# A four-layer hybrid trunk on one core: one-half norms and gating moved into PSUM, layer norm on VectorE alone, low halves gathered, and another final norm

## The chip, the cores and the metric

The kernel runs on one core of a Trainium2 chip. A core has a matrix engine (TensorE, PE in the profile, with its weight loads listed as PEld), a vector engine (VectorE, DVE), an activation engine (ScalarE, ACT), a general engine (GpSimd, POOL) and a queue engine (SyncE, SP). Each engine works through its own instructions in order. The metric is the device time of the kernel in microseconds (us), the median of several runs, lower is better.

## The reference

One inference step of a four-layer trunk with model width 1024, for a prompt of 512 positions and a sample group of 8 x 4 = 32 positions that share the weights. Each layer is a token mixer and a SwiGLU block, each with a norm ahead of it and a residual around it:

```python
for i in range(4):
    h = rmsnorm(x, norm_mix[i])
    # i=0 pooling, i=1 Conformer convolution (31 taps), i=2 gating MLP, i=3 gated short conv
    x = x + mixer_i(h)
    x = x + silu(gate) * up @ w_out        # gate, up = split(rmsnorm(x, norm_ffn[i]) @ w_in)
y = rmsnorm(x, norm_final)

def rmsnorm(x, g): return x * rsqrt(mean(x * x) + 1e-6) * g

def conv(h):                               # layer 1
    a, gate = split(h @ w_in + b_in)
    c = depthwise_causal(a * sigmoid(gate), dw) + dw_b
    return silu(layernorm(c)) @ w_out

def gating(h):                             # layer 2, chunks of 128 positions, 4 groups of 256 columns
    u, v = split(gelu(h @ w_in))
    v = layernorm(v)
    mixed = tril(w_s) @ v (per chunk and group) + b_s
    return (u * mixed) @ w_out
```

Everything is float32. The outputs are y and the new states of the mixers.

## The kernel before

**Tiling.** Activations lie feature-major: 8 tiles of 128 features (NC = 8), and the 544 positions are two halves, A (256 prompt positions) and B (256 prompt and 32 sample positions). A float32 product is three single-pass matmuls: each weight tile and each activation is split into a high part, cast by ACT (`hi_...`, `H_...`, `hH_...`), and a low part, raw minus high, by DVE or POOL (`lo_...`, `L_...`, `hL_...`); per 128x128 tile PE does high x high, high x low and low x high. In layers 2 and 3 (counted from 0) the SwiGLU block's inner pairs use seven products in the place of eight (`seven`).

**Order.** `Stream` holds the steps (one weight column each: loads, matmuls, evacuation) and writes every engine's instructions by hand: ahead of a step's matmuls the casts of weights up to four slots and the low halves up to three slots ahead; behind them one stage of each pending evacuation (generators: each `yield` is the end of a stage), then the side generators (the norms that are prepared), then background jobs (pool mixer, convolution taps, layer norm) as far as a cost model of DVE and POOL (`Timed`) says that they fit beside PE. A step with `flush` first writes out all pending evacuations. Raw weights come by SP's queue. A weight load with `share=True` has its low half on POOL unless the model finds POOL behind, with `share=0` on DVE; with `sum=True` ACT writes the negated high half and a DMA issued by POOL adds the raw weight from memory onto it (lines 173 to 178).

**PSUM** has eight banks, and every tile there is one bank, taken in turn (`PS`). SBUF tiles of 288 columns come from one pool (`T`).

**The norms** (lines 437 to 561). ACT squares each x tile, the squares are added over the eight tiles (`add_square`), matmuls with a column of ones sum over features into `st_...`, and `rsqrt_` makes the inverse root on a few columns by an integer first step and two polynomial steps. Where one half alone is normed (`twin`), part of its operands lie in PSUM, with three copies. `rp_...` matmuls spread the result over all partitions. `factor` keeps it as a factor for later; `prepare` norms the tiles at once, two a stage: DVE makes `hn`, ACT casts it in that stage, DVE and POOL make the low halves a stage later.

**Where the change applies, in order of time.** SwiGLU 0 runs for half A (about 26 to 237 us); then the convolution's input for A (`conv_in`, 237 to 286), SwiGLU 0 for B, the convolution's output for A, its input for B (521 to 575), SwiGLU 1 for A, and so on. The 31 taps (`conv_taps`) are a background job on DVE in PSUM accumulators; for B, four products with row sums add the sample positions, and POOL adds their bias and gathers the sum over the channel tiles (`gather`, called a tile later). The gating layer runs from about 1004 to 1177 us: 16 columns `ps_gv` (v first, then u), transposes of v, `gm_norm` as a background job (`vT`, five blocks of positions times four groups; blocks 0 and 2 have two of their steps on POOL, `LN_POOL`), and `mix_step` for each tile and half placed among the columns by `GM_A` and `GM_B`: matmuls `mix`, then `mix_evac` (`gy` = mix + bias, times u, cast to `H_gy`, and `L_gy` a stage later). `out_proj` for A then begins (`ps_go`). The last SwiGLU block takes its last two output columns (`tail=2`) first for A and then for B, so that A's final norm (`final`) runs beside B's columns; A's result tiles `y` are made by POOL, B's by DVE, and go out by SP's and ACT's queues.

Of the kernel before, what the change touches and what calls it, by code (L numbers as in the profile page):

```python
# [10 lines left out]
I32 = mybir.dt.int32  # L11
# [4 lines left out]
P = 128  # L16
# [55 lines left out]
def trunk_kernel(  # L72
# [364 lines left out]
    def rsqrt_(ms, wv, tv, twin=None):  # L437


        wp, tp = twin or (wv, tv)  # L440
# [5 lines left out]
        dve.tensor_scalar(tv.bitcast(I32), ms.bitcast(I32), 1, None, op0=ALU.logical_shift_right)  # L446
        dve.tensor_scalar(wv.bitcast(I32), tv.bitcast(I32), -1, 0x5F3759DF, op0=ALU.mult, op1=ALU.add)
# [14 lines left out]
    def token_rsqrt(acc, halves, name, lag, mid=(None,)):  # L462
# [8 lines left out]
        twin = (ps[:, 8 + b0 : 8 + b1], ps[:, 16 + b0 : 16 + b1]) if len(halves) == 1 else None  # L471
# [10 lines left out]
        for rows, c0, c1 in ((P, b0, min(b1, 4)), (NS, 4, b1)):  # L482
            if c1 > c0:
                dve.tensor_scalar(
                    ms[:rows, c0:c1], ps[:rows, c0:c1], 1.0 / D, EPS, op0=ALU.mult, op1=ALU.add
                )
        rsqrt_(*(t[:, b0:b1] for t in (ms, rs, tv)), twin)
# [13 lines left out]
    class Norm:  # L501
# [16 lines left out]
        def add_square(self, h, c, eng):  # L518
# [4 lines left out]
            elif eng is None:  # L523
                self.acc[h] = [self.acc[h], q]
            else:
# [17 lines left out]
        def prepare(self, h, eng):  # L543
# [5 lines left out]
            for c in range(0, NC, 2):  # L549
                vs = []  # L550
                for i in (c, c + 1):
# [5 lines left out]
                    self.hs[h][i] = split(v, w, f"h_{nm}_{i}")  # L557
                    vs.append(v)
                yield
                for i, v in zip((c, c + 1), vs):  # L560
                    split_lo(self.hs[h][i], v, w, dve if i % 2 else eng)
# [146 lines left out]
    def ffn(layer, n, nxt, halves=(0, 1), rel=False, fill=None, tail=0, free=False, phases=((0, HF), (HF, NF))):  # L708

        eng = pool if rel else dve  # L710
# [3 lines left out]
        for pi, (j0, j1) in enumerate(phases):  # L714
# [101 lines left out]
            for m in range(NC):  # L816
# [3 lines left out]
                if joint and not (final_phase and m >= NC - tail):  # L820
# [8 lines left out]
            for i, (m, hs) in enumerate(seq):  # L829
                if len(hs) == 1 and tail and hs[0] == B:  # L830
# [7 lines left out]
                    S.add(lds[m][:1], lambda wt, m=m, piece=piece: piece(wt, m, 0), lambda ps: iter(()))  # L838
                    S.add(lds[m][1:], lambda wt, m=m, piece=piece: piece(wt, m, (K + 1) // 2),
# [7 lines left out]
    def out_proj(src, acts, n, name, halves=(0, 1), rel=False, fill=None, between=None):  # L847
# [8 lines left out]
        for q in range(NC // 2):  # L856
            ls = cols_of(src[q], f"{name}_{q}_{hn}", bool(rel))
            for i, l in enumerate(ls):
# [213 lines left out]
    def conv_in(h, fill):  # L1072
# [65 lines left out]
        for c in range(NC):  # L1138
            la, lg = cols_of(w_cin[c], f"ci{c}_{h}", True)
# [12 lines left out]
    def conv_taps(h, c, e, ev):  # L1152
# [23 lines left out]
        if ev is not None:  # L1176
# [9 lines left out]
            pool.tensor_scalar(cc[:, HP:w], cc[:, HP:w], col(C_DWB + c), None, op0=ALU.add)  # L1186
        dve.tensor_add(cc[:, :HP], cc[:, :HP], outs[1])

        def gather():

            if c == 0:
# [129 lines left out]
    def gm_norm():  # L1321
# [11 lines left out]
        for g in range(NG):  # L1333
            for b, (h, o, n) in enumerate(blocks):
# [3 lines left out]
                if b in LN_POOL:  # L1338
                    dve.tensor_scalar(v, v, mu, r, op0=ALU.subtract, op1=ALU.mult)
# [329 lines left out]
```

## Time and profile before

| | us |
|---|---|
| median of 3 runs | 2135.81 (2133.74 to 2137.49) |
| the profiled execution, its own time | 2138.85 |
| its span, first to last instruction | 2137.2 |
| PE busy in the span | 2107.3 |
| DVE / ACT / POOL busy | 1485.7 / 1018.5 / 646.2 |

PE is busy in almost all of the span, and the rest of the span is waits of PE and stretches of a half granted clock. A matmul's start is exact, its end is modelled. The views used below are the page, the list of who waited for whom on PE, the timeline (start, length, engine, line, operation, output<-inputs, shapes, count, and in brackets the idle time ahead and what ended it), groups of instructions (count | busy us, mean ns | idle before), and windows (busy us of PE with the number of instructions, granted clock, DMA share, GB/s). Nearly all DVE, POOL and PE instructions bear line 109, that of a helper, so they are told apart by the names of their tiles.

### The profile page before, as it was taken

To read this page: it belongs to the slowest core of one execution; us is meant where nothing else is said; L and a number is where in the kernel's file an instruction comes from. 1 tells how busy PE (TensorE), PEld (TensorE's weight loads), DVE (VectorE), ACT (ScalarE), POOL (GpSimd) and SP (SyncE) were. 2 spreads that over 40 slices of the span, in tenths; PEclk is the share of its full clock that TensorE was granted. 3 is DMA by queue.
4 is the path that set the end of the run, shared out by engine and by line. 5 is a ranking of instruction groups with operands and counts; after the bars stand their busy time and mean duration, and the time that the engine had idled before them with its cause. 6 is when DMAs were issued, how large, how long until landed. Compare 5 with 4: busy or idle time off the path is not lost.

```text
span 2137.2 us, 42390 instructions
## 1 busy us (share of the span) xinstructions
PE 2107.3 (99%) x16678; PEld 2097.1 (98%) x16678; DVE 1485.7 (70%) x3191; ACT 1018.5 (48%) x1778; POOL 646.2 (30%) x502
## 2 busy tenths in 40 slices
PE   9999999999999999999999999999999999999997
PEld 8999999999999999999989999999999999999997
DVE  7867799624999666566387767586765649585685
ACT  5445544545444654444436546354521246364463
POOL 3011587879888840000043102011000001111121
PEclk9999999999999999999999999999999999999998
DMA  7645554545956465546225646465544455575562
GB/s 237 212 155 159 180 188 145 182 145 193 188 179 193 153 203 158 173 155 192 87 75 154 155 119 155 129 152 146 136 92 91 90 139 114 133 160 132 134 150 72
DMA packets 130190, 320.81 MB, mean 150 GB/s; under 512 B 32556, under 2 KB 40328, under 8 KB 129728
## 3 DMA queue, kind: packets, MB, share of 16 engines
q1 hardware_dynamic: 110664, 279.47, 44.2%
q0 software_dynamic: 18176, 37.33, 10.7%
q8 instruction: 131, 2.15, 0.4%
q10 hardware_dynamic: 1152, 1.32, 0.2%
q14 instruction: 67, 0.55, 0.1%
HBM read 313.81 MB, written 4.62 MB: 149 GB/s over the span
## 4 chain that ended last, share of the span: by engine, by line
PE 88%; DVE 7%; ACT 2%; DMA 2%; issue 1%; POOL 0%; ACTq 0%; DVEq 0%; POOLq 0%
PE ps_o L109 24%; PE p_w L109 18%; PE ps_g L109 12%; PE ps_u L109 12%; PE ps_gv L109 3%; PE ps_co L109 2%; PE ps_sx L109 2%; PE ps_sc L109 2%; PE ps_sbg L109 2%; PE ps_so L109 2%; PE ps_cg L109 2%; PE ps_ca L109 1%; DVE ct L109 1%; DMA raw_fi<-in_w_fin 1%; PE ps_go L109 1%; PE pd L109 1%
## 5 line engine op out<-in xcount | busy, mean ns | idle before, releaser
L109 PE MATMUL ps_o<-H_p,lo_fo 128*128 128x288 f32 (+1 forms) x1408 | 349.8, 288 | 1.4 <-POOL lo_fo L109 1.4
L109 PE MATMUL ps_o<-H_p,hi_fo 128*128 128x288 f32 (+1 forms) x1408 | 350.3, 288 | 0.0
L109 PE MATMUL ps_o<-L_p,hi_fo 128*128 128x288 f32 (+1 forms) x1408 | 349.6, 288 | 0.1
L169 ACT CAST hi_fi<-raw_fi 128x1024 fp32r<-128x1024 f32 x192 | 201.0, 1049 | 126.8 <-DMA raw_fi<-in_w_fin 47.9
L109 PEld LDWEIGHTS ps_o<-H_p,lo_fo 128*128 128x128 f32 x1408 | 245.7, 188 | 1.6 <-POOL lo_fo L109 1.6
L109 PEld LDWEIGHTS ps_o<-L_p,hi_fo 128*128 128x128 f32 x1408 | 245.8, 188 | 1.4 <-DVE L_p L109 1.4
L109 PEld LDWEIGHTS ps_o<-H_p,hi_fo 128*128 128x128 f32 x1408 | 245.9, 188 | 0.2
L169 ACT CAST hi_fo<-raw_fo 128x768 fp32r<-128x768 f32 (+2 forms) x194 | 149.8, 774 | 194.3 <-PE ps_o L109 106.2
L249 POOL DMA_DIRECT2D lo_w_a<-in_w_fin x92 | 80.7, 1002 | 443.2 <-ACT lo_w_a L248 425.8
L109 POOL TENSOR_TENSOR lo_fi<-raw_fi,hi_fi 128x1024 fp32r<-128x1024 f32 (+1 forms) x86 | 203.5, 2385 | 25.9 <-PE ps_g L109 6.7
L109 DVE TENSOR_TENSOR lo_fo<-raw_fo,hi_fo 128x768 fp32r<-128x768 f32 (+3 forms) x130 | 113.8, 878 | 121.4 <-issue 69.5
L109 DVE SCALAR_TENSOR_TENSOR ct<-ce,colsT,ct 128x256 f32<-128x256 f32 x448 | 182.8, 487 | 0.0
L109 DVE TENSOR_TENSOR lo_fi<-raw_fi,hi_fi 128x1024 fp32r<-128x1024 f32 (+1 forms) x92 | 116.4, 1267 | 64.1 <-ACT t L735 17.4
L109 PE MATMUL p_w<-L_t_f,hi_w_s 128*128 128x272 f32 x432 | 124.3, 288 | 0.0
L109 PE MATMUL p_w<-H_t_f,hi_w_s 128*128 128x272 f32 x432 | 124.1, 287 | 0.0
L109 PE MATMUL p_w<-H_t_f,lo_w_s 128*128 128x272 f32 x432 | 123.9, 287 | 0.0
L109 PE MATMUL ps_g<-hH_f,hi_fi 128*128 128x256 f32 (+1 forms) x464 | 123.7, 289 | 0.0
L109 PE MATMUL ps_u<-hH_f,hi_fi 128*128 128x256 f32 (+1 forms) x464 | 123.6, 289 | 0.0
L109 PE MATMUL ps_g<-hH_f,lo_fi 128*128 128x256 f32 (+1 forms) x464 | 123.2, 288 | 0.2 <-DVE lo_fi L109 0.2
L109 PE MATMUL ps_u<-hL_f,hi_fi 128*128 128x256 f32 (+1 forms) x464 | 123.3, 288 | 0.0
L109 PE MATMUL ps_u<-hH_f,lo_fi 128*128 128x256 f32 (+1 forms) x464 | 123.2, 288 | 0.0
L109 PE MATMUL ps_g<-hL_f,hi_fi 128*128 128x256 f32 (+1 forms) x464 | 123.1, 288 | 0.0
(430 smaller groups left out, 6675.5 us busy)
## 6 DMA issues: line engine op xcount, KB each, us to landing
raw_fi<-in_w_fin SPq DMA_DIRECT2D x192, 512.0 KB, 4.4
raw_fo<-in_w_fout SPq DMA_DIRECT2D x96, 384.0 KB, 3.2
raw_w<-in_w_fin SPq DMA_DIRECT2D x72, 512.0 KB, 4.2
raw_fo<-in_w_fout SPq DMA_DIRECT2D x94, 320.0 KB, 3.2
lo_w_a<-in_w_fin POOLq DMA_DIRECT2D x92, 256.0 KB, 4.9
raw_ci<-in_w_cin SPq DMA_DIRECT2D x32, 512.0 KB, 4.6
raw_co<-in_w_cout SPq DMA_DIRECT2D x16, 512.0 KB, 4.8
raw_gi<-in_w_gin SPq DMA_DIRECT2D x16, 512.0 KB, 3.9
```

The source lines that it names most:

```text
L109: return fn(*a, **k)
L169: act.copy(self.hi, self.raw)
L249: nc.gpsimd.dma_start(self.lo, self.pair.plain(self.k)[1], accum_op=ALU.add)
```

## The change

Ten edits. **(1)** `rsqrt_`: the integer step is one instruction in the place of two; for one half it reads a copy of `ms` in PSUM. **(2)** The sums of squares of SwiGLU 0's half A are added up in a PSUM tile (`eng = "psum"`). **(3)** `prepare` casts the normed tiles a stage later, with the low halves in that same stage. **(4)** The convolution's first two input columns for A have their low halves on DVE and not as POOL's share. **(5)** The sample bias of the convolution moves from the end of the taps into `gather`. **(6)** The layer norm of the gating MLP is all on DVE, two instructions per block and group. **(7)** The gating product stays in the PSUM tile of `mix` and is cast from there. **(8)** Columns 8 to 15 of the gating input have their low halves gathered (`sum`). **(9)** The first two output columns of the gating layer for A run as a pair: `mm_pair` takes both columns tile by tile and the low weights one tile later. **(10)** The end: three columns (`tail=3`) first for A and then for B, one load each; no PSUM twin in the last norm; `idle` matmuls ahead of and behind B's statistics; A's result on DVE and later.

```diff
@@ -437,14 +437,14 @@
-        wp, tp = twin or (wv, tv)
+        wp, tp, mp = twin or (wv, tv, ms)
...
-        dve.tensor_scalar(tv.bitcast(I32), ms.bitcast(I32), 1, None, op0=ALU.logical_shift_right)
-        dve.tensor_scalar(wv.bitcast(I32), tv.bitcast(I32), -1, 0x5F3759DF, op0=ALU.mult, op1=ALU.add)
+        dve.tensor_scalar(wv.bitcast(I32), mp.bitcast(I32), -0.5, float(0x5F3759DF), op0=ALU.mult, op1=ALU.add)
         copied(wp, wv)
@@ -459,7 +459,7 @@
-    def token_rsqrt(acc, halves, name, lag, mid=(None,)):
+    def token_rsqrt(acc, halves, name, lag, mid=(None,), alone=False):
@@ -468,7 +468,9 @@
         ms, rs, tv = (sp.tile([P, 5], F32, tag=f"n{n}", name=f"{n}_{name}", bufs=2) for n in ("ms", "ri", "rt"))
-        twin = (ps[:, 8 + b0 : 8 + b1], ps[:, 16 + b0 : 16 + b1]) if len(halves) == 1 else None
+        twin = None
+        if len(halves) == 1 and not alone:
+            twin = [ps[:, o + b0 : o + b1] for o in (8, 16, 24)]
         if B in halves:
@@ -484,6 +486,8 @@
                 )
+        if twin:
+            dve.tensor_copy(twin[2], ms[:, b0:b1])
         rsqrt_(*(t[:, b0:b1] for t in (ms, rs, tv)), twin)
@@ -522,6 +526,11 @@
                 self.acc[h] = [self.acc[h], q]
+            elif eng == "psum":
+                a = self.acc[h]
+                self.acc[h] = q if c == NC - 1 else PS(f"sa_{self.name}_{h}") if c == 1 else a
+                dve.tensor_add(self.acc[h][:, :w], a[:, :w], q[:, :w])
             else:
@@ -546,19 +555,24 @@
             yield
-            for c in range(0, NC, 2):
+            last = ()
+            for c in range(0, NC + 2, 2):
+                for i, v in last:
+                    self.hs[h][i] = split(v, w, f"h_{nm}_{i}")
                 vs = []
-                for i in (c, c + 1):
+                for i in range(c, min(c + 2, NC)):
                     v = (PS if i % 2 else T)(f"hn_{nm}_{i}")[:, :w]
...
                     )
-                    self.hs[h][i] = split(v, w, f"h_{nm}_{i}")
-                    vs.append(v)
+                    vs.append((i, v))
+                for i, v in last:
+                    split_lo(self.hs[h][i], v, w, dve if i % 2 else eng)
+                last = vs
                 yield
-                for i, v in zip((c, c + 1), vs):
-                    split_lo(self.hs[h][i], v, w, dve if i % 2 else eng)
@@ -707,7 +721,7 @@
-        eng = pool if rel else dve
+        eng = pool if rel else "psum" if halves == (A,) else dve
         hn = "".join(map(str, halves))
@@ -817,7 +831,7 @@
                 cut = ((j0, ks[0]), ks)
-                if joint and not (final_phase and m >= NC - tail):
+                if joint:
                     cut = ((j0, j1),)
@@ -835,8 +849,9 @@
-                    S.add(lds[m][:1], lambda wt, m=m, piece=piece: piece(wt, m, 0), lambda ps: iter(()))
-                    S.add(lds[m][1:], lambda wt, m=m, piece=piece: piece(wt, m, (K + 1) // 2),
+                    k1 = (K + 1) // 2
+                    S.add(lds[m], lambda wt, m=m, piece=piece: piece(wt[:k1], m, 0), lambda ps: iter(()))
+                    S.add(lds[m], lambda wt, m=m, piece=piece: piece(wt[k1:], m, k1),
                           lambda ps, m=m, hs=hs: out_evac(ps, m, hs, True))
@@ -844,7 +859,7 @@
-    def out_proj(src, acts, n, name, halves=(0, 1), rel=False, fill=None, between=None):
+    def out_proj(src, acts, n, name, halves=(0, 1), rel=False, fill=None, between=None, pair=False):
         hn = "".join(map(str, halves))
@@ -855,6 +870,13 @@
             ls = cols_of(src[q], f"{name}_{q}_{hn}", bool(rel))
+            if pair and q == 0:
+                S.add(ls, lambda wt: mm_pair((wt[:NC], wt[NC:]), acts, halves, name),
+                      lambda pss: both(evac(pss[0], 0), evac(pss[1], 1)), flush=True, fill=fill)
+                for m in range(2):
+                    if between:
+                        between(m)
+                continue
             for i, l in enumerate(ls):
@@ -1136,7 +1158,7 @@
         for c in range(NC):
-            la, lg = cols_of(w_cin[c], f"ci{c}_{h}", True)
+            la, lg = cols_of(w_cin[c], f"ci{c}_{h}", h == B or c > 1)
             if c == 0:
@@ -1183,11 +1205,12 @@
                 yield 0.7
-            pool.tensor_scalar(cc[:, HP:w], cc[:, HP:w], col(C_DWB + c), None, op0=ALU.add)
         dve.tensor_add(cc[:, :HP], cc[:, :HP], outs[1])
...
+            if ev is not None:
+                pool.tensor_scalar(cc[:, HP:w], cc[:, HP:w], col(C_DWB + c), None, op0=ALU.add)
             if c == 0:
@@ -1335,13 +1358,8 @@
                 mu, r = mv[:n, b, 0:1], rs[:n, b : b + 1]
-                if b in LN_POOL:
-                    dve.tensor_scalar(v, v, mu, r, op0=ALU.subtract, op1=ALU.mult)
-                    pool.tensor_mul(v, v, lg)
-                    pool.tensor_add(v, v, lb)
-                else:
-                    dve.scalar_tensor_tensor(v, v, mu, lg, op0=ALU.subtract, op1=ALU.mult)
-                    dve.scalar_tensor_tensor(v, v, r, lb, op0=ALU.mult, op1=ALU.add)
+                dve.scalar_tensor_tensor(v, v, mu, lg, op0=ALU.subtract, op1=ALU.mult)
+                dve.scalar_tensor_tensor(v, v, r, lb, op0=ALU.mult, op1=ALU.add)
                 if b == 3:
@@ -1367,33 +1385,31 @@
         w = HW[h]
-        y = T(f"gy_{c}_{h}")
         bs = gk["bs"]
-        dve.tensor_add(
-            b3(y[:, :HP], 2), b3(pmx[:, :HP], 2), bs[:, g : g + 1, :].to_broadcast([P, 2, CH])
-        )
+        y = b3(pmx[:, :HP], 2)
+        dve.tensor_add(y, y, bs[:, g : g + 1, :].to_broadcast([P, 2, CH]))
         if h == B:
-            dve.tensor_add(
-                b3(y[:, HP:w]), b3(pmx[:, HP:w]), bs[:, g : g + 1, :DS].to_broadcast([P, DB, DS])
-            )
-        dve.tensor_mul(y[:, :w], y[:, :w], uu[h][c][:, :w])
-        gact[h][c] = split(y[:, :w], w, f"gy_{c}_{h}")
-        return y
+            y = b3(pmx[:, HP:w])
+            dve.tensor_add(y, y, bs[:, g : g + 1, :DS].to_broadcast([P, DB, DS]))
+        dve.tensor_mul(pmx[:, :w], pmx[:, :w], uu[h][c][:, :w])
+        gact[h][c] = split(pmx[:, :w], w, f"gy_{c}_{h}")
     def mix_evacs(pss, hs, c):
-        ys = {h: mix_evac(pss[h], c, h) for h in hs}
+        for h in hs:
+            mix_evac(pss[h], c, h)
         yield
         for h in hs:
-            split_lo(gact[h][c], ys[h][:, : HW[h]], HW[h], dve)
+            split_lo(gact[h][c], pss[h][:, : HW[h]], HW[h], dve)
...
     for q in range(NC):
-        for i, l in enumerate(cols_of(w_gin[q], f"gi{q}", 0)):
+        for i, l in enumerate(cols_of(w_gin[q], f"gi{q}", 0, q >= NC // 2)):
             m = 2 * q + i
@@ -1409,7 +1425,7 @@
-    out_proj(w_gout, gact, nf2, "go", (A,), rel=True, between=mix_b)
+    out_proj(w_gout, gact, nf2, "go", (A,), rel=True, between=mix_b, pair=True)
     out_proj(w_gout, gact, nf2, "go", (B,))
@@ -1499,28 +1515,43 @@
     nl = Norm(C_FIN, "nl")
-    ffn(3, nf3, nl, fill=1, tail=2, phases=JOINT)
+    ffn(3, nf3, nl, fill=1, tail=3, phases=JOINT)
...
+    def idle(n):
+        ps = PS("idle")
+        for _ in range(n):
+            pe.matmul(ps[:, :P], ones, ones, start=True, stop=True)
...
         w = HW[h]
-        out = yield from token_rsqrt(nl.acc, (h,), f"nl_{h}", [None])
+        def covered(n):
+            if h == B:
+                idle(n)
+            yield
+        if h == B:
+            idle(4)
+        out = yield from token_rsqrt(
+            nl.acc, (h,), f"nl_{h}", covered(0) if h == B else [None] * 2, mid=covered(7), alone=True
+        )
         if h == A:
-            r = T(f"r_nl_{h}")
-            scaled(r[:, :w], out[h][:, :w])
+            for _ in range(3):
+                yield
         for c in range(NC):
-            y = T(f"y_{h}_{c}")
-            if h == A:
-                pool.tensor_mul(y[:, :w], xg[h, c][:, :w], r[:, :w])
-            else:
-                dve.scalar_tensor_tensor(
-                    y[:, :w], xg[h, c][:, :w], RSQ, out[h][:, :w], op0=ALU.mult, op1=ALU.mult
-                )
+            y = T(f"y_{h}_{c}")[:, :w]
+            dve.scalar_tensor_tensor(y, xg[h, c][:, :w], RSQ, out[h][:, :w], op0=ALU.mult, op1=ALU.mult)
             q = act if h == B and c % 2 == 0 else nc.sync
-            q.dma_start(o_y[c, :, HO[h] : HO[h] + w], y[:, :w])
+            q.dma_start(o_y[c, :, HO[h] : HO[h] + w], y)
+            if h == A and c == 2:
+                yield
@@ -1537,7 +1568,6 @@
 PAIRS = (1,)
-LN_POOL = (0, 2)
 GM_A = {11: (0, 1), 12: (2, 3), 13: (4,), 14: (5, 6), 15: (7,)}
```

## The prediction, made before the changed kernel was run

> **What bounds the kernel now.** First the page, for the share of PE; then the list of who ended PE's waits; then windows around the longest of these, for the granted clock; then the timeline there, for the cause.
>
> ```profile
> PE 2107.3 (99%) x16678; PEld 2097.1 (98%) x16678; DVE 1485.7 (70%) x3191; ACT 1018.5 (48%) x1778; POOL 646.2 (30%) x502
> ```
>
> ```profile
> PE rp_nl L109 <- DVE ri_nl L109: 4.0, 2, 3.4
> PE pd L109 <- DVE ht L109: 3.9, 1, 3.9
> PE ps_go L109 <- ACT H_gy L608: 3.4, 1, 3.4
> PE mix L109 <- DVE vT L109: 2.0, 1, 2.0
> PE ps_cg L109 <- ACT ct L1083: 1.6, 1, 1.6
> PE ps_o L109 <- POOL lo_fo L109: 1.4, 1, 1.4
> ...
> PE ps_cga L109 <- ACT hH_n L530: 1.1, 1, 1.1
> ...
> PE ps_cg L109 <- DVE ct L109: 0.9, 1, 0.9
> ```
>
> ```profile
> 547.20:550.60 3.40, 1.82 (x14) 1.00 0.95 253
> 1100.10:1103.50 3.40, 3.40 (x18) 0.55 0.26 87
> 1124.00:1127.40 3.40, 3.40 (x17) 0.55 0.02 6
> 2124.10:2137.20 13.10, 3.49 (x16) 0.50 0.47 161
> ```
>
> PE is idle for 2137.2 - 2107.3 = 29.9 us in all, and the matmuls themselves stay (the pairing only reorders them). So an edit counts only where it ends one of these waits, or a stretch at half clock. The windows add a second price: behind the waits of 2.0 and 3.4 us PE had some 3.4 us at half clock (0.55 in windows a little off its edges), so each cost about another 3.4 x 0.5 = 1.7 us; the wait of 1.6 us, whose window kept 1.00, cost only itself.
>
> [...]
>
> **The change, part by part, in order of time.**
>
> *Start.* `pd` waits on the pool mixer's norm, where `rsqrt_` loses one of its small instructions, about 0.2 us apart (below). **0.2 us.**
>
> *Convolution input, A.*
>
> ```profile
> 231.68 10.03 POOL L109 TENSOR_TENSOR lo_ci<-raw_ci,hi_ci 128x1024 fp32r<-128x1024 f32 x4 [47.48 <-PE ps_o L109]
> 239.38 2.61 DVE L109 TENSOR_TENSOR sq_n<-sq_n,sq_n 128x256 f32<-128x256 f32 x1
> 540.74 5.57 DVE L109 SCALAR_TENSOR_TENSOR ct<-ce,colsT,ct 128x256 f32<-128x256 f32 x14
> 541.23 2.42 POOL L109 TENSOR_TENSOR lo_ci<-raw_ci,hi_ci 128x1024 fp32r<-128x1024 f32 x1 [0.52 <-issue]
> ```
>
> The sum of squares took 2.61 us beside POOL's low halves and ends when POOL's instruction ends; the taps, which accumulate in PSUM, took 5.57 / 14 = 0.40 us each beside the same kind of POOL instruction. So a DVE instruction on SBUF alone stands still beside POOL, and one with an operand in PSUM does not. Edits 2 and 4 take away both sides: the sums go to PSUM, and the first four low halves to DVE, 4 x 1.22 us (row `lo_gi` below, same shape). POOL's four in a row each held up one DVE instruction, this one by 2.61 - 0.45 = 2.2 us, and the last x, whose cast PE waits for, stands behind them. Counting only the last two, 4.3 us go, and the two low halves that come ahead of the last x bring 2.4: DVE is 1.9 us earlier where PE waits 1.05. **1.05 us**; if DVE were as late as now, nothing. The integer steps of edit 1 are unblocked too, but `rp_n` stands at a fixed place in PE's order, so the next wait, 0.9 us `<- DVE ct` (a bank that waits for r), stays: 0.
>
> *Convolution input, B, and SwiGLU 1, A.*
>
> ```profile
> 547.28 0.77 ACT L608 CAST H_h_f<-hn_f 128x256 fp32r<-128x256 f32 x2 [3.64 <-DVE hn_f L109]
> 656.97 0.36 POOL L109 TENSOR_SCALAR cc<-cc,colsT 128x32 f32<-128x32 f32 x1 [5.46 <-DVE cc L109]
> 657.29 6.67 POOL L109 TENSOR_TENSOR lo_fo<-raw_fo,hi_fo 128x768 fp32r<-128x768 f32 x4
> ```
>
> ACT stood 3.64 us at the cast of `hn_f`, with the sigmoid that frees PE's bank behind it. A stage later `hn_f` is long done, so ACT doesn't stop. What is late next is DVE: its low halves now share a stage with the casts and may wait for them, in a stretch where DVE has hardly a pause. Between nothing and the whole 1.6 us I take half, **0.8 us**; below nothing it could go to about -2 (each of four stages losing the 0.5 us that a cast takes to arrive). POOL stood 5.46 us at the sample bias, four low halves behind it, and PE's 1.4 us wait ended with the first. In `gather`, a tile later, the taps are done, so the bias waits for nothing: **1.4 us**.
>
> *The gating layer.*
>
> ```profile
> L109 DVE TENSOR_TENSOR lo_gi<-raw_gi,hi_gi 128x1024 fp32r<-128x1024 f32 x16 | 19.6, 1224 | 34.8 <-issue 20.5 <-PE ps_gv L109 12.8 <-PE ps_o L109 1.5
> L109 DVE TENSOR_TENSOR L_gy<-gy,H_gy 128x256 fp32r<-128x256 f32 (+1 forms) x16 | 16.9, 1057 | 5.6 <-ACT H_gy L608 5.6
> L109 DVE SCALAR_TENSOR_TENSOR vT<-vT,mv,lng 128x256 f32<-128x256 f32 (+1 forms) x12 | 9.8, 813 | 0.0
> L109 DVE TENSOR_SCALAR vT<-vT,mv,gri 128x256 f32<-128x256 f32 x8 | 3.6, 455 | 0.0
> L109 DVE TENSOR_TENSOR ps_u<-ps_u,t 128x288 f32<-128x288 f32 (+1 forms) x42 | 18.8, 446 | 31.0 <-PE ps_u L109 27.7 <-ACT t L732 3.3
> L109 DVE TENSOR_TENSOR q<-q,t 128x256 f32<-128x256 f32 (+1 forms) x60 | 26.3, 449 | 6.0 <-DVE q L109 0.9 <-ACT t L735 0.9
> L109 POOL TENSOR_TENSOR vT<-vT,lng 128x256 f32<-128x256 f32 x8 | 6.8, 844 | 82.1 <-DVE vT L109 79.6 <-issue 1.2 <-DMA out<-vT 1.2
> L109 POOL TENSOR_TENSOR lo_go<-raw_go,hi_go 128x1024 fp32r<-128x1024 f32 x8 | 19.9, 2492 | 12.1 <-ACT hi_go L169 8.4 <-PE ps_go L109 3.6
> L176 ACT ACTIVATE lo_fi<-hi_fi 128x1024 fp32r<-128x1024 f32 x16 | 16.9, 1057 | 19.9 <-issue 16.2 <-PE ps_so L109 2.5 <-PE ps_go L109 1.2
> L177 POOL DMA_DIRECT2D lo_fi<-in_w_fin x16 | 13.9, 870 | 118.7 <-ACT lo_fi L176 109.5 <-DVE x L109 9.3
> ```
>
> DVE is the late one: both waits come from its queue. It gains: the low halves of columns 14 and 15, which fall among the norm's instructions, 2 x 1.22 = 2.4 us (six more fall where DVE has pauses); `L_gy` at 0.45 for a mean of 1.06, and up to 2 us where it met `lo_go`; and the norm no longer meets 16 POOL instructions of 0.8 us. It loses: eight `vT` of 0.455 become sixteen of 0.41 to 0.81, so 8 x (0.82 - 0.455) = 2.9 up to 8 x (1.63 - 0.455) = 9.4 us. I take 4, since most of the POOL instructions that made the 0.81 are gone. `lo_go` stays on POOL and will meet the norm instead of `L_gy`; so up to the first wait (1097.5 us) the gain is the 2.4, plus about 3 for the norm's and gating's stalls, less 5/8 of the 4: about 3 us, against the 2.0 that PE waits. Up to the second, 1.6 us more from the `L_gy` just ahead of it and the rest of the stalls, together some 5; and the pair lets PE do 40 instead of 21 matmuls, 19 x 0.126 = 2.4 us more (2107.3 us by 16678 matmuls), before it needs the last `H_gy`. That is 7.4 us of cover for the 3.4. So both waits and both half-clock stretches go: 2.0 + 1.7 + 3.4 + 1.7 = **8.8 us**; the first has only about 1 us in hand. The gathered columns cost ACT 8 x 1.06 and POOL 8 x 0.87 us, both off the path: a column's low half is begun three columns of 48 x 0.126 = 6.0 us ahead.
>
> [...]
>
> *The end.*
>
> ```profile
> 1.13 6.11 PE L109 MATMUL warm<-ones 128*128 128x128 f32 x40 [1.13 <-DVE ones L109]
> 2118.30 0.16 DVE L109 TENSOR_SCALAR ms_nl<-st_nl 128x2 f32<-128x2 f32 x1 [1.52 <-PE st_nl L109]
> 2120.91 0.71 PE L109 MATMUL rp_nl<-ident,ri_nl 128*128 128x128 f32 x4 [0.57 <-DVE ri_nl L109]
> 2122.12 0.29 PE L109 MATMUL ps_o<-H_p,lo_fo 128*128 128x288 f32 x1
> 2123.09 0.45 DVE L109 TENSOR_TENSOR x<-ps_o,x 128x288 f32<-128x288 f32 x1
> 2124.06 1.75 PE L109 MATMUL st_nl<-ones,sq_nl 128*128 128x1 f32 x10 [0.46 <-ACT sq_nl L516]
> 2129.25 1.78 PE L109 MATMUL rp_nl<-ident,ri_nl 128*128 128x128 f32 x6 [3.44 <-DVE ri_nl L109]
> 2131.07 3.01 DVE L109 SCALAR_TENSOR_TENSOR y<-xg,rp_nl 128x288 f32<-128x288 f32 x8 [1.87 <-PE rp_nl L109]
> ```
>
> The last column ends at 2122.12 + 0.29 = 2122.41; from there 14.8 us to the end of the span. To the statistics 1.65: the residual started 0.68 late on DVE; with A's chain over earlier it is about 1.0, but four `idle` matmuls of 6.11 / 20 = 0.31 stand ahead, so 1.2. Statistics 1.75 at half clock, about 1.0 when `idle` holds the clock. Chain 3.44 for 13 instructions: A's twelve took 2120.91 - 2118.30 = 2.61, 0.22 each; ten remain and no POOL stands beside them, 2.2, plus 0.2 since A's last five `y` precede them on DVE. The seven `idle` matmuls, 2.1, fit beside that. Spreading 1.82, about 1.0 at full clock. The results and their way out, 6.1, stay. 1.2 + 1.0 + 2.4 + 1.0 + 6.1 = 11.7, so 3.1 us less; and A's 0.57 us wait goes, its spreading now two pieces of a column later. **3.6 us.**
>
> **Sum.** 0.2 + 1.05 + 0.8 + 1.4 + 8.8 + 3.6 = 15.85 us, from the profiled 2138.85 to 2123.0. The median of the runs is 2135.81, 3.04 below the profiled execution; with the same distance the forecast is 2120.0.
>
> **Rivals.** *The norm keeps DVE late.* With `lo_go` on POOL beside a longer norm, the first wait stays (only it: 15.85 - 3.7 = 12.15, 2123.7 us) or both (7.05, 2128.8). For it: only about 1 us in hand. Against the second: cover twice its need. *PSUM doesn't shield.* If the cast and low halves from PSUM stand still as those from SBUF do, gating and convolution A win nothing: 0.2 + 0.8 + 1.4 + 3.6 = 6.0, 2129.8 us. The taps' 0.40 speak against it. *Other waits fill in*, within 0.2% (4.3 us, about what a measurement here can tell from no change): new waits of 12 us or more, say DVE late in the convolution, 2133. *Slower: the gathered halves come late.* PE needs a column's low half at its third matmul, so each of eight columns can stall. They have 18 us; ACT's 1.06, POOL's 0.87 and a transfer must fit. It decides from 18 on: 1.8 us beyond, with half clock behind each wait, 8 x 3.5 = 28 us against the 15.85, so about 2148. Against it: the windows show the DMA engines at 0.02 to 0.26 in that stage.
>
> **How the numbers follow.** Forecast 0.62 (2115.5 to 2122.5: banks and small waits that also go, or 2.5 us of the end or of the convolution not won), first gating wait stays 0.13, both stay 0.07, no shield 0.05, filled in 0.07, slower 0.06. The range of 8 in 10 goes from 2115.5 to 2127.5: the forecast, the next case and part of the third. Faster by over 0.2%: 0.62 + 0.13 + 0.07 + 0.05 = 0.87; within 0.07; slower 0.06.
>
> **What would show it.** Right: no PE wait on `H_gy`, `vT`, `lo_fo` or `hH_n`, granted clock 1.00 from 1090 to 1130 us and up to the last `rp_nl`, `L_gy` near 0.45 us, some 12 us from the last `ps_o` to the end of the span, and the 0.9 us wait on `ct` still there. Wrong: a PE wait on `lo_gi`, on `L_gy` or `L_h`, or a `mix` that still waits on `vT`; `idle` matmuls that hold up `rp_nl`.

## The result, and the profile after

The changed kernel takes 2125.09 us (median of 6 runs, 2120.3 to 2130.03) beside 2137.59 us for the kernel before in the same rounds (6 runs, 2133.74 to 2142.48): a ratio of 0.9939, 95% interval 0.9925 to 0.9952. A second set of rounds on another occasion gave 2122.61 (6 runs) beside 2133.91 (11 runs), again 0.9939 (0.992 to 0.9958). The forecast was 2120.0 in a range of 2115.5 to 2127.5, so the time lies inside the range and the gain is 12.5 us where 15.85 was forecast. The profiled execution took 2125.66, its span 2124.0; 13.2 us of span went, and the profiles tell where.

The page of the changed kernel, its line of busy times:

```profile
PE 2105.0 (99%) x16700; PEld 2096.3 (99%) x16700; DVE 1450.7 (68%) x3186; ACT 1021.6 (48%) x1783; POOL 617.9 (29%) x482
```

PE has 22 matmuls more, the 11 `idle` ones in two passes each, and is idle for 2124.0 - 2105.0 = 19.0 us, before 29.9. Who ended its waits (us in total, times, longest):

```profile
PE mix L109 <- DVE vT L109: 2.4, 2, 2.2
PE ps_g L109 <- ACT hi_fi L169: 2.4, 1, 2.4
PE pd L109 <- DVE ht L109: 2.1, 1, 2.1
...
PE ps_cg L109 <- DVE ct L109: 0.9, 1, 0.9
...
PE ps_g L109 <- DVE lo_fi L109: 0.8, 1, 0.8
...
PE rp_nl L109 <- DVE ri_nl L109: 0.2, 1, 0.2
...
PE ps_go L109 <- ACT H_gy L622: 0.2, 1, 0.2
```

The waits on `hH_n`, `ct` by ACT and `lo_fo` are gone, that on `H_gy` is 0.2 for 3.4, those on `ri_nl` are 0.2 for 4.0, and the 0.9 on `ct` by DVE is still there: as forecast, but for the 0.2 us on `H_gy`. The wait of `mix` on `vT`, which was to go, is 2.4 for 2.0. Windows of the changed kernel (its columns as before) around the start, the gating layer and the end:

```profile
57.00:60.20 3.20, 0.82 (x5) 0.42 (x3) 0.51 (x1) 1.59 (x3) 0.00 (x0) 0.99 0.70 277
60.20:67.00 6.80, 6.04 (x29) 6.03 (x29) 6.59 (x12) 4.79 (x7) 0.00 (x0) 0.50 0.60 183
1098.80:1103.40 4.60, 2.17 (x16) 1.69 (x14) 4.50 (x10) 2.01 (x4) 1.39 (x1) 1.00 0.42 132
1110.91:1116.06 5.15, 4.99 (x42) 4.78 (x41) 3.38 (x10) 2.79 (x7) 2.41 (x1) 1.00 0.07 17
2112.52:2123.97 11.45, 4.83 (x41) 4.32 (x39) 6.64 (x26) 0.87 (x2) 0.00 (x0) 0.91 0.59 197
```

The clock was full (1.00) through the gating layer and up to the last matmul, which ended at 2117.59 us: the 0.91 of the last window is half clock from 2121.81 us on. The timeline of the changed kernel, for the norm of convolution input B (534 us), for the gating layer and for the end:

```profile
533.82 2.40 POOL L109 TENSOR_TENSOR lo_ci<-raw_ci,hi_ci 128x1024 fp32r<-128x1024 f32 x1 [1.06 <-issue]
534.21 0.16 DVE L109 TENSOR_SCALAR ri_f<-st_f 128x2 int32<-128x2 int32 x1
...
1085.76 2.39 POOL L109 TENSOR_TENSOR lo_go<-raw_go,hi_go 128x1024 fp32r<-128x1024 f32 x1 [0.46 <-PE ps_gv L109]
1085.77 2.64 DVE L109 SCALAR_TENSOR_TENSOR vT<-vT,gri,lnb 32x256 f32<-32x256 f32 x1
1093.57 2.40 POOL L109 TENSOR_TENSOR lo_go<-raw_go,hi_go 128x1024 fp32r<-128x1024 f32 x1 [5.43 <-ACT hi_go L169]
1093.72 2.53 DVE L109 SCALAR_TENSOR_TENSOR vT<-vT,mv,lng 128x256 f32<-128x256 f32 x1
1098.51 0.47 DVE L109 SCALAR_TENSOR_TENSOR vT<-vT,mv,lng 128x256 f32<-128x256 f32 x1
1102.29 1.27 PE L109 MATMUL mix<-gk,vT 128*128 128x128 f32 x8 [2.19 <-DVE vT L109]
1116.06 0.39 PE L109 MATMUL ps_go<-H_gy,hi_go 128*128 128x256 f32 x1 [0.16 <-ACT H_gy L622]
...
2112.36 1.05 PE L109 MATMUL idle<-ones 128*128 128x128 f32 x8
2113.25 1.34 PE L109 MATMUL st_nl<-ones,sq_nl 128*128 128x1 f32 x12
2114.63 0.21 DVE L109 TENSOR_SCALAR ms_nl<-st_nl 128x2 f32<-128x2 f32 x2
2116.57 1.01 PE L109 MATMUL rp_nl<-ident,ri_nl 128*128 128x128 f32 x6 [0.23 <-DVE ri_nl L109]
2117.62 3.01 DVE L109 SCALAR_TENSOR_TENSOR y<-xg,rp_nl 128x288 f32<-128x288 f32 x8 [1.20 <-PE rp_nl L109]
```

Each stage's length, from the first matmul of its first column to that of the next stage in the two timelines, gives the account of the span:

| stage | before | after | gained | forecast for it |
|---|---|---|---|---|
| up to the convolution's input, A | 237.03 | 237.21 | -0.18 | 0.2 |
| convolution input, A | 48.80 | 47.49 | 1.31 | 1.05 |
| convolution input, B | 53.56 | 51.74 | 1.82 | 0.8 |
| SwiGLU 1, A | 95.77 | 94.52 | 1.25 | 1.4 |
| gating input | 112.46 | 111.26 | 1.20 | gating together 8.8 |
| gating output | 60.32 | 55.08 | 5.24 | |
| last output columns to the end of the span | 47.49 | 43.27 | 4.22 | 3.6 |
| all other stages | 1481.72 | 1483.40 | -1.68 | 0 |

This account rests on one profile of each kernel. That of the kernel before spent 10.24 + 3.41 + 3.41 + 13.4 = 30.5 us of its span at half clock (start, gating layer twice, end), a mean granted clock of 0.993. Seven of its eleven executions in the second set have 0.995 or 0.996 on record, by an estimate from that mean 17 to 21 us at half clock. So in most of these some of the stretches at the start or in the gating layer were not there; which ones, no profile shows.

### The profile page after: what moved, and what is told of

It reads as the page before. It is cut to its first block, busy times and chain, and to the rows that moved or that the text cites. A ratio compares the mean times of both kernels' runs of the same rounds, so it can differ in the third digit from the quotient of the medians.

```text
span 2124.0 us, 42395 instructions
## 1 busy us (share of the span) xinstructions
PE 2105.0 (99%) x16700; PEld 2096.3 (99%) x16700; DVE 1450.7 (68%) x3186; ACT 1021.6 (48%) x1783; POOL 617.9 (29%) x482
## 4 chain that ended last, share of the span: by engine, by line
PE 90%; DVE 6%; DMA 1%; ACT 1%; issue 1%; POOL 0%; DVEq 0%; ACTq 0%; POOLq 0%
PE ps_o L109 25%; PE p_w L109 18%; PE ps_g L109 13%; PE ps_u L109 12%; PE ps_gv L109 3%; PE ps_co L109 2%; PE ps_sx L109 2%; PE ps_sc L109 2%; PE ps_sbg L109 2%; PE ps_so L109 2%; PE ps_cg L109 2%; PE ps_ca L109 2%; DMA raw_fi<-in_w_fin 1%; PE ps_go L109 1%; DVE vT L109 1%
## 5 line engine op out<-in xcount | busy, mean ns | idle before, releaser
L169 ACT CAST hi_fo<-raw_fo 128x768 fp32r<-128x768 f32 (+1 forms) x192 | 149.4, 780 | 188.9 <-PE ps_o L109 107.5
L109 DVE TENSOR_TENSOR lo_fo<-raw_fo,hi_fo 128x768 fp32r<-128x768 f32 (+1 forms) x128 | 113.5, 889 | 121.0 <-issue 66.6
```

Source lines behind the costliest of these rows:

```text
L109: return fn(*a, **k)
L169: act.copy(self.hi, self.raw)
```

## The experiments

Twelve kernels ran; all but the last are the changed kernel with the edit shown. Single times scatter by several us, most of it from the start, whose stages no edit aims at; so what these kernels show is read from stages and waits. Beside x1 to x4 the kernel before took 2140.1 us, beside x5 to x8 2133.04, beside x9 to x12 2133.91 (median of 11). Where no number of runs is given, it was one.

| kernel | us | gating input | gating output | convolution input B |
|---|---|---|---|---|
| changed, first profile | 2125.66 | 111.26 | 55.08 | 51.74 |
| x12_changed | 2122.61 (6 runs) | 112.77 | 54.32 | 51.74 |
| x1_no_pair | 2124.71 | 112.73 | 55.86 | 51.74 |
| x2_gate_sbuf | 2127.89 | 114.06 | 58.63 | 51.74 |
| x3_ln_pool | 2127.01 | 115.63 | 54.26 | 51.74 |
| x4_no_gather | 2126.0 | 114.30 | 54.31 | 51.74 |
| x5_pool_lo_no_idle | 2121.05 | 112.75 | 54.13 | 51.89 |
| x6_sums_sbuf_early_cast | 2122.5 | 113.02 | 54.13 | 51.71 |
| x7_bias_early_twin | 2125.96 | 112.87 | 54.31 | 51.74 |
| x8_go_gather | 2122.66 | 108.32 | 59.25 | 51.74 |
| x9_int_sbuf | 2128.03 | 112.80 | 54.31 | 53.29 |
| x10_int_sbuf_early_cast | 2123.39 | 112.79 | 54.17 | 53.51 |
| x11_go_gather_two | 2121.65 (6 runs) | 108.32 | 54.31 | 51.74 |

### The convolution

**x6_sums_sbuf_early_cast** takes back the sums in PSUM and the later casts:

```diff
-        eng = pool if rel else "psum" if halves == (A,) else dve
+        eng = pool if rel else dve
...
-            for c in range(0, NC + 2, 2):
-                for i, v in last:
-                    self.hs[h][i] = split(v, w, f"h_{nm}_{i}")
+            for c in range(0, NC, 2):
...
+                    self.hs[h][i] = split(v, w, f"h_{nm}_{i}")
```

> Two edits undone, read at their own places. Edit 2 (sums of squares of half A in SBUF, low halves still on DVE): with nothing on POOL beside them the sums take 0.42 us and no wait on hH_n comes back, so edit 4 alone carries this place; rival: the wait of about 1 us comes back. Edit 3 (normed tiles cast in their own stage): my theory is that ACT stands at H_h_f again and PE's wait of 1.6 us in the convolution input of B comes back; rival: that wait came from elsewhere, no wait.

Neither wait came back: convolution input A 47.48 us (changed 47.49), B 51.71 (51.74). So low halves on DVE (edit 4) are enough for A without sums in PSUM, and the theory that the later casts (edit 3) removed the wait in B fell. ACT stood only 0.90 us at the same cast, 3.64 before:

```profile
541.58 0.77 ACT L619 CAST H_h_f<-hn_f 128x256 fp32r<-128x256 f32 x2 [0.90 <-DVE hn_f L109]
```

(timeline of x6). The tiles themselves came earlier. In the kernel before, the timeline of DVE shows why they were late:

```profile
535.09 2.22 DVE L109 TENSOR_SCALAR rt_f<-ms_f 128x2 int32<-128x2 int32 x1
537.34 0.17 DVE L109 TENSOR_SCALAR ri_f<-rt_f 128x2 int32<-128x2 int32 x1
```

The first integer step, two columns wide, took 2.22 us where its neighbour took 0.17. In the changed kernel it reads PSUM and took 0.16 at 534.21, in the middle of a POOL instruction of 2.40 us. So the new theory was edit 1, and two kernels tested it.

**x9_int_sbuf** puts only the integer step back on SBUF:

```diff
-        dve.tensor_scalar(wv.bitcast(I32), mp.bitcast(I32), -0.5, float(0x5F3759DF), op0=ALU.mult, op1=ALU.add)
+        dve.tensor_scalar(wv.bitcast(I32), ms.bitcast(I32), -0.5, float(0x5F3759DF), op0=ALU.mult, op1=ALU.add)
...
-        if twin:
-            dve.tensor_copy(twin[2], ms[:, b0:b1])
```

> The integer step of the one-half norms on SBUF again (one instruction, no copy into PSUM); all else as changed. New theory for the wait of 1.6 us in the convolution input of B: the integer step stood still beside POOL for 2.2 us and put the normed tiles late, so ACT stood at their cast; edit 1 took that away, and edit 3 is enough too. Then here, with edit 3 kept, rt_f's place is slow again (about 2 us in one instruction) but no PE wait of over 0.3 us comes back. Rival: edit 1 alone is the cause, and 1 to 1.6 us come back.

**x10_int_sbuf_early_cast** has that edit and the casts in their old stage (the part of x6 that concerns `prepare`):

> Edits 1 (integer step) and 3 (cast a stage later) both undone. New theory: either is enough alone, so only with both undone ACT stands 3 us or more at H_h_f and PE's wait of 1.2 to 1.6 us in the convolution input of B is back. Rival: neither has to do with it, no wait.

The stage became 1.55 us longer in x9 and 1.77 in x10. The timeline of x9:

```profile
534.09 2.40 POOL L109 TENSOR_TENSOR lo_ci<-raw_ci,hi_ci 128x1024 fp32r<-128x1024 f32 x1 [1.06 <-issue]
534.30 2.21 DVE L109 TENSOR_SCALAR ri_f<-ms_f 128x2 int32<-128x2 int32 x1
...
551.59 0.37 PE L109 MATMUL ps_ca<-H_h_n,hi_ci 128*128 128x288 f32 x1 [1.31 <-DVE ce L109]
```

and of x10:

```profile
542.99 0.40 PE L109 MATMUL ps_cg<-H_h_n,hi_ci 128*128 128x288 f32 x1 [1.35 <-ACT ct L1100]
```

One two-column instruction moved back to SBUF is held until POOL's ends (534.30 + 2.21 = 536.51; 534.09 + 2.40 = 536.49), and PE loses 1.3 us again. The expectation that either edit alone is enough fell: it is edit 1 alone. Edit 3 only chooses through whom the delay reaches PE, DVE's `ce` or ACT's `ct`.

**x5_pool_lo_no_idle** takes back the low halves on DVE (edit 4) and leaves out the `idle` matmuls:

```diff
-            la, lg = cols_of(w_cin[c], f"ci{c}_{h}", h == B or c > 1)
+            la, lg = cols_of(w_cin[c], f"ci{c}_{h}", True)
...
-            idle(4)
+            idle(0)
...
-            nl.acc, (h,), f"nl_{h}", covered(0) if h == B else [None] * 2, mid=covered(7), alone=True
+            nl.acc, (h,), f"nl_{h}", covered(0) if h == B else [None] * 2, mid=covered(0), alone=True
```

> Two edits undone, 1900 us apart, each read at its own place. Edit 4 (the convolution's first low halves for A are POOL's again, the sums stay in PSUM): my theory is that hL_n, on SBUF alone, still stands still beside POOL, so 0.3 to 1.0 us of the wait on hH_n comes back; rival: the sums in PSUM did it alone, no wait. The idle matmuls of edit 10 left out: my theory is that the last statistics and the last spreading run at half clock, 0.8 to 1.2 us more from the end of the last column to the end of the span (11.4 us with them); rival: the clock holds or those matmuls are bound by their issue, then the same or 0.2 us less.

Convolution input A took 47.50 us: the sums in PSUM alone are enough too. With x6, either of edits 2 and 4 removes this wait. From the end of the last column to the end of the span x5 took 11.79 us, the changed kernel 11.45. In the eleven profiles that keep this end, though, that stretch runs from 11.45 to 12.14 us, and the difference lies in the way out behind the last `y` (3.33 to 4.03 us). Up to the first `y` they agree, 5.10 to 5.12 us, and x5 took 5.43: the clock that `idle` holds is worth 0.33 us, less than was expected. Spreading took 1.46 us for 1.05. The statistics did not slow down, since in x5 the granted clock fell only at 2111.95 us, within the spreading.

### The sample bias and the last norm

**x7_bias_early_twin**:

```diff
                 yield 0.7
+            pool.tensor_scalar(cc[:, HP:w], cc[:, HP:w], col(C_DWB + c), None, op0=ALU.add)
...
-            if ev is not None:
-                pool.tensor_scalar(cc[:, HP:w], cc[:, HP:w], col(C_DWB + c), None, op0=ALU.add)
...
-            nl.acc, (h,), f"nl_{h}", covered(0) if h == B else [None] * 2, mid=covered(7), alone=True
+            nl.acc, (h,), f"nl_{h}", covered(0) if h == B else [None] * 2, mid=covered(7)
```

> Two edits undone, read at their own places. Edit 5 (sample bias at the end of the taps): my theory is that POOL stands at it again and PE waits 1 to 2 us on a low half in SwiGLU 1, A; rival: POOL's low halves fit anyway, no wait. Of edit 10 the last norm has its PSUM twin again: four small copies more, 4 x 0.2 = 0.8 us more from the last column to the end of the span; rival: the chain is hidden by A's last result tiles on DVE, under 0.3 us.

Its list of PE's waits:

```profile
PE rp_nl L109 <- DVE ri_nl L109: 1.0, 1, 1.0
...
PE st_nl L109 <- ACT sq_nl L520: 0.8, 1, 0.8
...
PE ps_g L109 <- POOL lo_fi L109: 0.7, 1, 0.7
...
PE ps_o L109 <- POOL lo_fo L109: 0.2, 1, 0.2
```

The bias put back costs 0.9 us of waits on POOL's low halves, a little under the expected 1 to 2; against x12 the kernel is 1.5 us later from there on (SwiGLU 1, A, and the stage behind it). The twin put back costs 1.6 us at the end (13.05 for 11.45, and as much up to the first `y`), twice what was expected: its four copies lengthen not only B's chain (0.8) but A's before it on DVE's queue, which shows as the wait of 0.8 on `sq_nl`. The rest of edit 10 (three last columns, one load each, A's result on DVE) was not taken back by itself.

### The gating layer

**x1_no_pair** (edit 9 undone):

```diff
-    out_proj(w_gout, gact, nf2, "go", (A,), rel=True, between=mix_b, pair=True)
+    out_proj(w_gout, gact, nf2, "go", (A,), rel=True, between=mix_b)
```

> Edit 9 undone: the first two output columns of the gating layer run one after the other. My theory: the pair is what hides the last H_gy, since PE then comes to it after 21 and not 40 matmuls, 2.4 us earlier, and after the change it already arrives just in time (0.16 us wait): PE waits 2.4 to 2.6 us on H_gy, with up to 1.7 us more where a window at half clock follows. Rival: the relief of DVE alone did it, then the wait stays under 0.5 us.

**x2_gate_sbuf** (edit 7 undone):

```diff
-        y = b3(pmx[:, :HP], 2)
-        dve.tensor_add(y, y, bs[:, g : g + 1, :].to_broadcast([P, 2, CH]))
+        y = T(f"gy_{c}_{h}")
+        dve.tensor_add(
+            b3(y[:, :HP], 2), b3(pmx[:, :HP], 2), bs[:, g : g + 1, :].to_broadcast([P, 2, CH])
+        )
...
-        dve.tensor_mul(pmx[:, :w], pmx[:, :w], uu[h][c][:, :w])
-        gact[h][c] = split(pmx[:, :w], w, f"gy_{c}_{h}")
+        dve.tensor_mul(y[:, :w], y[:, :w], uu[h][c][:, :w])
+        gact[h][c] = split(y[:, :w], w, f"gy_{c}_{h}")
```

> Edit 7 undone: the gating product lies in SBUF again. My theory: L_gy and the product stand still beside POOL's lo_go again (L_gy mean 0.9 us or more, 0.43 after the change); since three lo_go meet the layer norm either way, the waits on vT stay near 2.4 us, and the H_gy wait grows to 1.5 to 2.5 us; the stage loses 2 to 4 us. Rival: every lo_go holds one DVE instruction whichever it is, so nothing moves (under 0.5 us).

**x3_ln_pool** (edit 6 undone):

```diff
+                if b in (0, 2):
+                    dve.tensor_scalar(v, v, mu, r, op0=ALU.subtract, op1=ALU.mult)
+                    pool.tensor_mul(v, v, lg)
+                    pool.tensor_add(v, v, lb)
+                else:
```

> Edit 6 undone: two of five blocks of the layer norm have their last two steps on POOL again. My theory: POOL's 16 instructions hold DVE up by more than the 8 x 0.5 = 4 us that they save it, so PE's waits on vT grow from 2.4 to 3.5 us or more. Rival: DVE has less to do, and the waits on vT fall under 1 us.

**x4_no_gather** (edit 8 undone):

```diff
-        for i, l in enumerate(cols_of(w_gin[q], f"gi{q}", 0, q >= NC // 2)):
+        for i, l in enumerate(cols_of(w_gin[q], f"gi{q}", 0)):
```

> Edit 8 undone: DVE makes the low halves of the gating input's columns 8 to 15 again. My theory: the two that fall among the layer norm put DVE back 2.4 us, and the waits on vT grow from 2.4 to about 4.5 us, with 1.7 us more for a half clock window. Rival: these low halves lie where DVE waits for PE anyway, no change (under 0.5 us).

What PE waited for in the layer, from the lists of waits. In x1:

```profile
PE ps_go L109 <- ACT H_gy L622: 0.9, 1, 0.9
```

In x2:

```profile
PE mix L109 <- DVE vT L109: 2.5, 2, 2.2
...
PE ps_go L109 <- ACT H_gy L622: 1.8, 1, 1.8
...
PE ps_go L109 <- DVE L_gy L109: 0.6, 1, 0.6
```

In x3:

```profile
PE ps_gv L109 <- DVE L_gy L109: 1.9, 1, 1.9
PE mix L109 <- DVE L_gy L109: 1.7, 1, 1.7
```

In x4:

```profile
PE mix L109 <- DVE vT L109: 4.3, 1, 4.3
```

Each of the four edits earns something, but none of them frees `vT`. Both gating stages together take 167.09 us in x12, and 168.59 in x1, 172.69 in x2, 169.89 in x3 and 168.61 in x4, stretches at half clock included. Without the gathered halves the wait is 4.3 us, as expected; with the norm partly on POOL it is 3.7, as expected, and shows at `L_gy` and a bank. Without the gating in PSUM the waits up to `vT` are the same 2.5, and 2.4 more come at the output's columns for B; the loss is more than the 2 to 4 us expected. Without the pair the wait on `H_gy` is 0.9, not the 2.4 or more expected. In x1 half clock followed the `vT` wait (0.55 in the window from 1099.80 to 1103.60 us), which it did not in the first profile, and that gave DVE time; x12, with the pair and the same half clock, has no wait on `H_gy` at all.

**x8_go_gather** takes the other side away, POOL's low halves `lo_go`, with all eight output columns for A gathered like the input's:

```diff
-            ls = cols_of(src[q], f"{name}_{q}_{hn}", bool(rel))
+            ls = cols_of(src[q], f"{name}_{q}_{hn}", bool(rel), pair)
```

> The changed kernel, and the eight low halves of the gating output's weights for A gathered too (ACT's negated high half and a DMA that adds the weight), so that no POOL low half stands beside the layer norm. My theory: the three vT instructions of 2.5 to 2.6 us fall to 0.48, some 6 us of DVE, and PE's remaining waits on vT (2.4 us) and H_gy (0.16) go: 2.5 us less to the end of the stage. Rival: ACT, with 8 x 1.06 us more, is late with H_gy, and a wait of 1 us or more stands on H_gy or hi_go instead.

The gating input took 108.32 us, 2.94 less, with no wait on `vT`: without POOL's low halves beside the norm, nothing of the wait is left. But the output took 4.17 more, as the list of waits of x8 shows:

```profile
PE ps_go L109 <- DMA lo_go<-in_w_gout: 4.0, 3, 2.6
```

The gathered halves come late there. The input's columns take 6 us each and never waited; the output's for one half have half the work. The expected rival, ACT late with `H_gy` or `hi_go`, did not come. How long a gathered half took from issue to landing (median us, at the end of the row) stands in the DMA view of x8:

```profile
lo_go<-in_w_gout POOLq DMA_DIRECT2D x8, 512.0 KB, 7.7
```

**x11_go_gather_two** gathers only the first four of these columns, whose low halves are made while the input still runs:

```diff
+            ls = cols_of(src[q], f"{name}_{q}_{hn}", bool(rel), pair and q < 2)
```

> The changed kernel with the low halves of the gating output's first four weight columns for A gathered, the other four on POOL. My theory: the gating input's stage is 2.9 us shorter (108.3 us instead of 111.3), as with all eight gathered, and the output columns after the pair find their low halves in time (55 us to the next block instead of 59.3), so the kernel is 2 to 4 us faster than the changed one. Rival: POOL's low halves, now later, meet DVE or come late in the output stage and eat it, 0 to 1 us.

**x12_changed** is the changed kernel once more, in the same rounds:

> The changed kernel once more, on the same chip and in the same rounds as the one before it: a ratio to the kernel before of 0.993 to 0.995, and a start that ends (first output column of SwiGLU 0) anywhere from 86.5 to 92 us, since it varies from run to run with the half clock and the weights' transfers.

In x11 PE has no wait in the layer and keeps its clock, as a window over the second half of its input columns shows:

```profile
1075.00:1115.00 40.00, 40.00 (x320) 39.20 (x319) 31.73 (x81) 20.90 (x38) 8.42 (x8) 1.00 0.60 146
```

The norm's instructions take 482 and 474 ns where they took 591 and 682. The groups of the changed kernel in the span of the layer:

```profile
L109 DVE SCALAR_TENSOR_TENSOR vT<-vT,mv,lng 128x256 f32<-128x256 f32 (+1 forms) x20 | 13.6, 682 | 0.0
L109 DVE SCALAR_TENSOR_TENSOR vT<-vT,gri,lnb 128x256 f32<-128x256 f32 (+1 forms) x20 | 11.8, 591 | 0.7
...
L109 DVE TENSOR_TENSOR L_gy<-mix,H_gy 128x256 fp32r<-128x256 f32 (+1 forms) x16 | 7.0, 439 | 6.3 <-ACT H_gy L622 6.3
```

and of x11:

```profile
L109 DVE SCALAR_TENSOR_TENSOR vT<-vT,gri,lnb 128x256 f32<-128x256 f32 (+1 forms) x20 | 9.6, 482 | 0.7
L109 DVE SCALAR_TENSOR_TENSOR vT<-vT,mv,lng 128x256 f32<-128x256 f32 (+1 forms) x20 | 9.5, 474 | 0.0
```

The layer takes 108.32 + 54.31 = 162.63 us beside 166.34 and 167.09 in the two profiles of the changed kernel. In the rounds x11 took 2121.65 us, 0.9929 of before (0.9913 to 0.9945), x12 2122.61, 0.9939 (0.992 to 0.9958). The intervals overlap: that x11 is the faster kernel is shown in its layer, about 4 us, not in its time.

With x8 and x11 as the stage without a wait, the gating input can be accounted for: 108.32 us, plus its waits, plus 1.71 for each stretch of 3.41 us at half clock that the trace shows in it. That gives 108.32 + 1.98 + 1.71 = 112.0 for before (measured 112.46), 110.8 for the changed kernel (111.26), 112.5 for x12 (112.77), 114.2 for x2 with two stretches (114.06), 115.4 for x3 with two (115.63) and 114.3 for x4 (114.30).

## Why the prediction was right, and where it was not

**The direction, the path and most terms held.** Every gain lay where a wait of PE had been. Convolution input A gained 1.31 for a forecast 1.05, with its cause doubly provided for. The bias in `gather` gained 1.25 for 1.4; the stage varies by more than that among the profiles that keep the edit (93.3 to 96.0 us), so the edit's worth rests on the waits and on x7. The end, from the last column on, took 11.45 us for a forecast 11.7: the chain on DVE begins 2.11 after the column (forecast 1.2 + 1.0) and takes 1.94 (2.4), spreading 1.05 (1.0), results and their way out 6.35 (6.1). The term is larger than forecast, 4.2 for 3.6: 3.3 for 3.1 behind the last column and 0.9 for 0.57 ahead of it; what gave the rest, no run shows. `idle`, to which the working gave most of two steps, earns 0.33 of it (x5), the twin's missing copies 1.6 (x7).

**Step that failed: the first gating wait.** The sum has "both waits and both half-clock stretches go". The second wait and its stretch did; the first wait did not. It moved from the fifth `mix` to the seventh and became 2.4 us. That no half clock followed it in the first profile was luck, and the stage's gain of 1.20 us is no more than that: x12 and seven variants have the same wait of 2.19 us with half clock behind it, and in x12 the gating input takes 112.77 us, where the kernel before took 112.46. The working saw the mechanism ("`lo_go` stays on POOL and will meet the norm instead of `L_gy`") and had the right sum for it: the norm's instructions grew from 23.0 to 25.4 us in all. But it spread this over the stage, five eighths of it up to the wait. The timeline shows it in lumps, 2.64 for 0.47 at 1085.77 and 2.53 for 0.47 at 1093.72, together 4.2 us, in DVE's queue ahead of what PE waits for; x8 and x11 took these away and the wait went with them. The working also asked only whether the wait at its old place would go, not what PE's relief does: in the kernel before, the wait and the half clock behind it gave DVE 3.7 us for the tiles after it. So this is the rival "the first wait stays", at 2123.7, to which 0.13 was given, and the time lies inside the range because the range took that case in.

What standing beside POOL cost shows in the rows of single instructions: `vT` took 0.48 alone and 2.5 to 2.6 beside `lo_go`, the integer step 0.16 from PSUM and 2.21 from SBUF. Why a step of two columns with one input is held as long as a tile, no run shows. Such a stall has to be placed instruction by instruction; a mean (0.64 us over the 40 of `vT`) doesn't tell whom it hits.

**Mis-sized: the second gating wait.** "7.4 us of cover for the 3.4" was too much: 0.16 us of the wait were left in the first profile, so all of the cover was used. The first wait's DVE time was not won, and the lumps took the rest; this is argued from the timeline. The pair, priced at 2.4 us, is worth 0.9 us of wait behind a half-clock stretch (x1); without such a stretch it was not taken back.

**Step that failed: the cause in convolution input B.** It was put down to the casts a stage later, at half of 1.6 us. They earn nothing that x6, x9 and x10 could show (0.03, and 0.22 us between x9 and x10). The wait went since the integer step reads PSUM and is no longer held up by POOL for 2 us, an edit which the working priced at nothing there; the gain was 1.82. That this term had the right direction was luck. The row of 2.22 us was in the trace of before, and the working looked at A's chain alone.

**The start and the rest.** The start's 0.2 us cannot be seen. Before, it ran from 26.99 us to 91.84 at the first output column; after, from 21.16 to 91.89, since PE then waited 2.38 and 0.76 us for weights and spent 6.8 us at half clock (the first two windows). In the twelve other profiles this mark lies between 86.8 and 92.1 us, though little or nothing differs up to there. That is most of the scatter between the profiled times. Layers 2 and 3 behind the gating output lost 1.9 us without a new wait; the variants lost 0.7 to 2.3 there, against one profile of before. What sets this pace stays open.

## What to carry to other kernels

Price a stall beside POOL by its place, not by a mean: list which VectorE instruction will stand beside each POOL instruction, and ask what PE waits for behind that one; here a two-column step was held for 2.2 us, as long as a whole tile. Count a half-clock stretch behind a wait as a chance and not as a price. When one wait goes, look at what that wait had been giving time to, since the next tiles of the same queue inherit the lateness. Gathering low halves by DMA takes their making off both engines (an issue of 0.86 us stays on POOL), but it fits only where a column lasts long enough for the transfer: here columns of 6 us, whose halves took 6.8 us from issue to landing, had no wait, and columns of 3 us, with 7.7, had 4.0 us of waits (x8).

## What the runs showed of the hardware that was not expected

A wait near 2 us sometimes costs another 1.7 us and sometimes not. The `vT` wait of 2.2 us, at the same step of the same kernel, was followed by 3.41 us at half clock in x12 and by none in the first profile; the 2.58 us wait of x8 was followed by none. The window behind the wait in x12, where the first profile has 1.00:

```profile
1101.50:1104.90 3.40, 3.40 (x17) 3.40 (x16) 3.29 (x8) 0.00 (x0) 0.25 (x1) 0.50 0.11 39
```

Within each of the fourteen profiles all changes of the granted clock lie on one grid of 3.413 us, to 0.004 us, and only its offset differs from profile to profile. In the kernel before, the changes stand at 10.88, 21.12, 1099.74, 1103.15, 1123.63, 1127.04 and 2123.74 us: 0, 3, 319, 320, 326, 327 and 619 cells behind the first. PE's idle time within one cell of this grid (by the modelled ends) is what went with the half clock. In the kernel before, cells with 3.41, 2.69, 1.98 and 1.51 us idle were followed by it, cells with 1.58 and 1.45 were not; in the first profile of the changed kernel the cell with 2.38 was, that with 1.36 was not. Of all the cells that began at full clock with matmuls still to come, all 19 with more than 1.67 us idle were followed by half clock, and none with less than 1.38 us was; of the 12 between, seven were. The first profile's wait lies across a boundary, 1.36 us of idle time in one cell and 1.07 in the next; in x12 one cell has 1.49, in x8 the two have 0.91 and 1.66. So the offset, which differs even between the two profiles of the changed kernel, has more say in whether a wait near 2 us is paid for once more than the wait's length. What decides between 1.38 and 1.67 us stays open.

The gating product took 0.43 us at 256 columns and 0.47 at 288 from PSUM, as from SBUF where no POOL instruction stood in its way (0.43 and 0.46 before). Moving the tensor to PSUM cost DVE next to nothing here (a bias addition a mean of 347 ns for 334), and the rows of one product in the kernel before agree: `ps_u` 0.446 us in PSUM, `q` 0.449 in SBUF. Beside `lo_go` its instructions kept their time: `L_gy` took 0.46 us at 1113.17 and at 1122.21, in the middle of a POOL instruction of 2.4 us, where in the kernel before it took 2.0.
